# Two transposed probability tiles in one buffer, moved by four transfers, and the first gate weights loaded ahead of the late input rows

## The chip, the cores and the metric

The kernel runs on one core of one Trainium2 chip. The time is that of the device in microseconds (us); the kernel before takes 1884.54 us, the median of three runs (1883.9 to 1887.2). The engines named below are TensorE (PE), which does the matmuls, VectorE (DVE), ScalarE (ACT), GpSimd (POOL) and SyncE (SP), which issues nearly all DMA transfers from one queue, in order.

## The reference

One layer of an encoder is applied to two groups, "prompt" and "sample", of 1024 positions and 1024 channels each, with the same weights. All is in float32.

```
h    = rms_norm(x) * (1 + scale) + shift          # scale, shift, gate from silu(c) @ w_ada
proj = h @ w_in                                   # 1024 x 5376, cut into the parts below
# branch A: 8 query heads, 2 key/value heads, 64 wide; norm and rotation of q, k
oa = softmax(qa @ ka.T / 8) @ va  * silu(za)
# branch B: 4 heads, two 64-wide softmax maps each, 128-wide values
p  = softmax(q0 @ k0.T / 8) - lam * softmax(q1 @ k1.T / 8)
ob = rms_norm(p @ vb) * (1 - lam_init) * silu(zb)
merged = sigmoid(ga) * (oa @ w_proj_a) + sigmoid(gb) * (ob @ w_proj_b)
y = x + gate * (merged @ w_out)
```

## The kernel before, in words

Weights are split into a high part (rounded to the matmul's type, a step of ScalarE, L208) and a remainder (VectorE, L209), and most products are made of several matmuls of such parts. A buffer pool `st` of three tiles receives the weights from memory.

The program takes the prompt group (g = 0) and then the sample group (g = 1). Each has these stages, told with the times of the profiled execution for the prompt group: an opening with the input's norm, keys and values (0 to 130 us; in the sample group the input is normed earlier, behind the end of the prompt group, in `ht_gen`), branch A's attention (131 to 455), branch B's (510 to 808), and the merge with the output projection (about 771 to 972). The sample group's attention stages are at 1054 to 1340 and 1396 to 1714, and its output ends the program. While a stage of attention runs, projections of the next stage and the gate projections (`z_gen`) run beside it: they are matmuls L670 and L881 in the profile, and they fill TensorE while the softmax goes through the other engines. The merge is L1170 and the output L1201.

A **unit** of attention treats two tiles of 128 queries. A unit of branch A has two scores, one tile of probabilities for each of two heads; two units are needed for one mixing (`a_values`, L984). A unit of branch B has four, two maps for each of two query tiles, and is mixed by itself (`b_values`, L1021). For each score (`softmax_unit`) TensorE writes 128 x 1024 scores into one of two banks `s` (L908, L909), VectorE takes the row maximum (L910), ScalarE scales it (L911) and takes the exponential into a tile `p` (L912), which frees the bank. In branch B, VectorE combines the two maps (L952) with a factor `r` (L939, L940). In `flip`, VectorE transposes `p` in blocks of 32 x 32 (L953), and SP then issues four DMA transfers (L958, `q<-p`) that put the four groups of 32 partitions in their places in a tile `q`, from which TensorE takes the transposed probabilities. There are five buffers `p` of 4 KB a partition and two buffers `q` of 8 KB. The pool `p` also serves the opening, the gate loads of the merge (`p<-zd`, L1161), `ht_gen` and a few rows.

What sets the order: `weave` takes steps from several generators by their progress, with numbers from the tables at the top of the file (`ATT_W`, `IN_A`, `Z_A`, `LAST_ATT`, `TAIL` and others), and this gives the program order. A scheduler that simulates the program's timeline then places each instruction on its engine. Some instructions have a priority (`high_priority`, with `QUARTER_P` for instance). On the chip each engine works through its own list in that order.

In the opening, L109 is the line of a helper that keeps instructions in the order in which they are written. The late rows of the input (`load_xT0(1)`) are read there, and the weights of the first gate (`load_w`, into two tiles `u`), behind them.

## Time and profile before

| | us |
|---|---|
| median of three runs | 1884.54 |
| the profiled execution | 1887.84 |
| its span | 1885.6 |
| TensorE busy | 1852.3 (98%) |
| VectorE busy | 1228.1 (65%) |
| ScalarE busy | 843.1 (45%) |

The profiled execution's own time is the span and 2.24 us that lie around it. A view of waits has a row for each pair of waiting line and releaser: total us, times, and the longest. A timeline has start, duration, engine, line, operation, output and inputs, and in brackets the idle time before it with what ended it; `x4` is a run of four instructions that are shown as one. For SP a DMA row is the time of its issue, not of the transfer. In the list of DMA issues the last number is the median us from issue to landing.

### The profile page before, as it was taken

The numbers are of one execution on the slowest core, as the hardware profiler recorded it, in microseconds if no ns is written. First come the engines' busy times: TensorE is split into PE (matmuls) and PEld (weight loads), VectorE is DVE, ScalarE is ACT, GpSimd is POOL, SyncE is SP. The second block draws the span as 40 slices with busy tenths as digits, with TensorE's granted clock in tenths as the row PEclk, the third lists the DMA queues.
The fourth block names the chain that finished last, engine by engine and source line by source line (L and its number), as shares of the span: only waits on it lengthen the run. The fifth ranks groups of instructions, "written<-read, shape, count | busy, mean of one in ns | idle before, by whom it ended". The sixth has DMA issues, their size and how long they took to land.

```text
span 1885.6 us, 32132 instructions
## 1 busy us (share of the span) xinstructions
PE 1852.3 (98%) x11516; PEld 1599.4 (85%) x11516; DVE 1228.1 (65%) x1904; ACT 843.1 (45%) x1801; POOL 364.2 (19%) x692
## 2 busy tenths in 40 slices
PE   9999999999999999999999999999999999999999
PEld 7888888877889998788889888888888989877887
DVE  4756776465478677877464777666547767786731
ACT  3544554443456555524223555444445545552210
POOL 0342200011335152100134210000233513210000
PEclk9999999999999999999999999999999999999999
DMA  9225676676254536887531467776524344579532
GB/s 333 83 72 138 162 201 180 173 215 166 71 134 105 130 91 182 254 286 236 190 122 51 127 180 197 196 181 179 158 78 121 98 107 115 156 230 302 168 106 78
DMA packets 277612, 299.54 MB, mean 159 GB/s; under 512 B 37648, under 2 KB 228304, under 8 KB 277456
## 3 DMA queue, kind: packets, MB, share of 16 engines
q1 hardware_dynamic: 277456, 297.51, 55.6%
q8 instruction: 92, 1.51, 0.3%
q14 instruction: 64, 0.52, 0.1%
HBM read 137.91 MB, written 42.04 MB: 95 GB/s over the span
## 4 chain that ended last, share of the span: by engine, by line
PE 76%; DMA 7%; DVE 7%; SPq 3%; issue 3%; POOL 2%; ACT 2%; DVEq 0%; ACTq 0%; POOLq 0%
PE f L881 21%; PE f L670 18%; PE f L1201 6%; PE a L984 6%; PE f L1170 5%; PE s L908 5%; PE s L909 5%; PE a L1021 4%; PE s L1201 3%; DMA row<-zd 2%; PE s L1170 2%; DVE m L910 2%; SPq L958 1%; SPq L109 1%; DMA st<-in_w_in_dram 1%
## 5 line engine op out<-in xcount | busy, mean ns | idle before, releaser
L881 PE MATMUL f<-u,w 128*128 128x512 f32 x2088 | 524.9, 394 | 0.3 <-DVE u L733 0.3
L670 PE MATMUL f<-w,u 128*128 128x256 f32 x3264 | 448.2, 285 | 0.3 <-ACT ev L863 0.3
L881 PEld LDWEIGHTS f<-u,w 128*128 128x128 f32 x2088 | 382.7, 188 | 76.0 <-PE f L730 0.7
L670 PEld LDWEIGHTS f<-w,u 128*128 128x128 f32 x3264 | 425.2, 191 | 18.4 <-issue 1.4
L910 DVE TENSOR_REDUCE m<-s 128x1 f32<-128x1024 f32 x256 | 309.7, 1218 | 112.6 <-PE s L909 110.6
L953 DVE STREAM_TRANSPOSE p<-p 128x1024 f32<-128x1024 f32 x192 | 238.5, 1242 | 45.8 <-ACT p L912 42.1
L909 PE MATMUL s<-u,sw 128*128 128x512 f32 x512 | 202.9, 398 | 0.0
L209 DVE TENSOR_TENSOR w<-st,w 128x512 fp32r<-128x512 f32 x184 | 123.3, 699 | 82.4 <-ACT w L208 81.8
L208 ACT ACTIVATE w<-st 128x512 fp32r<-128x512 f32 x184 | 107.6, 626 | 133.5 <-DMA st<-in_w_in_dram 60.6
L912 ACT ACTIVATE p<-s,m,rsA 128x1024 f32<-128x1024 f32 x128 | 154.4, 1206 | 5.7 <-DMA q<-p 2.2
L912 ACT ACTIVATE p<-s,m,rsB 128x1024 f32<-128x1024 f32 x128 | 154.4, 1206 | 4.0 <-DMA q<-p 0.5
L695 POOL TENSOR_TENSOR rsB<-ss,nhalf 128x4 f32<-128x4 f32 x64 | 66.4, 1038 | 457.0 <-DVE ss L694 442.7
L1170 PE MATMUL f<-u,w 128*128 128x512 f32 x588 | 142.4, 391 | 0.2 <-DVE u L1181 0.2
L1021 PE MATMUL a<-q,u 128*128 128x256 f32 x512 | 126.1, 388 | 7.5 <-DMA q<-p 4.1
L1170 PEld LDWEIGHTS f<-u,w 128*128 128x128 f32 x588 | 109.9, 188 | 23.6 <-DVE u L1181 0.6
L984 PE MATMUL a<-q,u 128*64 128x128 f32 x2048 | 121.8, 276 | 4.0 <-DMA q<-p 3.9
L984 PEld LDWEIGHTS a<-q,u 128*64 128x64 f32 x2048 | 113.2, 138 | 14.6 <-issue 13.3
L733 DVE TENSOR_TENSOR u<-f,u 64x256 fp32r<-64x256 f32 (+1 forms) x208 | 83.7, 407 | 62.8 <-ACT u L732 57.5
L1021 PEld LDWEIGHTS a<-q,u 128*128 128x128 f32 x512 | 96.6, 194 | 23.0 <-issue 5.3
L1201 PE MATMUL f<-u,w 128*128 128x512 f32 x480 | 111.2, 389 | 0.0
L909 PEld LDWEIGHTS s<-u,sw 128*128 128x128 f32 x512 | 96.6, 189 | 16.2
L908 PE MATMUL s<-u 128*128 128x512 f32 x256 | 107.2, 421 | 2.6 <-ACT p L912 2.5
(208 smaller groups left out, 2152.1 us busy)
## 6 DMA issues: line engine op xcount, KB each, us to landing
q<-p SPq DMA_DIRECT2D x768, 128.0 KB, 2.8
st<-in_w_in_dram SPq DMA_DIRECT2D x128, 256.0 KB, 3.2
zd<-ev SPq DMA_DIRECT2D x96, 256.0 KB, 2.3
sw<-u SPq DMA_DIRECT2D x256, 64.0 KB, 2.1
p<-zd SPq DMA_DIRECT2D x64, 256.0 KB, 5.1
u<-in_w_ada_dram SPq DMA_DIRECT2D x16, 512.0 KB, 8.8
od<-oo SPq DMA_DIRECT2D x64, 128.0 KB, 2.6
st<-in_w_in_dram SPq DMA_DIRECT2D x64, 128.0 KB, 2.9
```

The source lines that it names most:

```text
L209: nc.vector.tensor_tensor(out=wl, in0=st, in1=wh.bitcast(F32), op=ALU.subtract)
L670: nc.tensor.matmul(ps, lt[c][:, sl], w[c][:, wi, :], start=(k == 0), stop=(k == 23))
L881: nc.tensor.matmul(ps, w[c][:, wi, e * P : (e + 1) * P], rt[c], start=(k == 0), stop=(k == 23),)
L908: nc.tensor.matmul(s[:, sl], q, k[:, sl], start=True, stop=False)
L909: nc.tensor.matmul(s[:, sl], sw, k[:, sl], start=False, stop=True)
L910: nc.vector.tensor_reduce(out=m, in_=s, axis=AX.X, op=ALU.max, negate=True)
L912: nc.scalar.activation(pt.rearrange("p (j c a) -> p j c a", j=4, c=8), s.rearrange("p (c a j) -> p j c a", c=8, j=4), AF.Exp, scale=rs, bi ...
L953: nc.vector.transpose(pt, pt)
L984: nc.tensor.matmul(acc[e * 64 : e * 64 + 64, n * P : n * P + P], u["v"](k), blocks[n][:, e, k], start=(k == 0 and n == 1), stop=(k == 7 an ...
L1021: nc.tensor.matmul(acc, u["v"][:, k], pT[:, k], start=(k == 0), stop=(k == 7))
L1170: nc.tensor.matmul(ps, w[:, c, wi, d * P : (d + 1) * P], o[:, oi, :], start=(k == 0), stop=(k == 11))
L1201: nc.tensor.matmul(ps, w[c][:, wi, e * P : (e + 1) * P], m[:, mi, :], start=(k == 0), stop=(k == 23))
```

## The change

There are now two buffers `p` of 8 KB (`p2tile`) and one single buffer `p1` of 4 KB. The two tiles of a unit (in branch B those of the first map, which also receive the combination) share one `p` buffer, laid out as 4 x 2 x 256; the second map of branch B goes into `p1`. The exponential writes with a stride, the transposition reads and writes with one, and `flip` issues nothing for the first tile; after the second, four transfers of 256 KB move both. So there are 384 transfers `q<-p`, not 768, and 863 rows on SP, not 1021. The helpers that used single `p` tiles take halves or quarters of a pair; the gate loads of the merge are issued four at once, one branch's into a `u` tile and the other's into a `p` pair (32 `u<-zd` and 32 `p<-zd` rather than 64 `p<-zd`). In the opening, three loads of the first gate's weights stand ahead of the late rows. The tables have other numbers. The matmuls are the same in number and shape. In the changed file the same places have other line numbers: L908 is L941, L912 is L945, L958 is L994, L984 is L1020, L1021 is L1057, L1170 is L1207, L764 is L797, L868 is L901, L991 is L1027, L208 is L215.

```diff
@@ -41,31 +41,31 @@
 Z_HEAD = (7, 6)
 Z_HEAD_A = (-0.216, -0.32)
 ATT_W = (
-    (0.893, 1.067, 1.068, 1.192, 1.03, 1.769),
-    (1.237, 1.862, 1.041, 1.418, 0.645, 1.256),
+    (0.893, 1.067, 1.068, 1.192, 0.961, 1.769),
+    (1.237, 1.635, 1.041, 1.418, 0.645, 1.256),
 )
 IN_A = (
-    (0.205, -0.07, 0.861, 0.05, 0.25, 0.15),
-    (0.125, -0.05, 0.368, 0.3, -0.03, 0.694),
+    (0.205, -0.07, 1.273, 0.05, 0.25, 0.15),
+    (0.125, -0.05, 0.435, 0.3, -0.03, 0.694),
 )
 Z_A = (
-    (0.2, 0.05, 0.62, -0.05, -0.1, -0.05),
+    (0.153, 0.05, 1.012, -0.05, -0.1, -0.05),
     (-0.215, 0.07, 0.2, 0.16, -0.3, -0.1),
 )
-LAST_ATT = (46, 40)
+LAST_ATT = (48, 40)
 LAST_FILL = (20, 25)
-GATED_A = (0.063, -0.144)
-LATE_A = 1.197
-QUARTER_P = 202
+GATED_A = (0.056, -0.144)
+LATE_A = 1.154
+QUARTER_P = 200
 KV_STEPS = 12
 GATE_AT = 6
 FIRST_ATT = 12
-FIRST_A = 0.26
-TAIL = (3, 3)
-TAIL_A = (0.92, 1.2)
+FIRST_A = 0.349
+TAIL = (1, 4)
+TAIL_A = (0.904, 1.2)
 LAG = 2
-Z_FIRST = (12, 6)
-Z_FIRST_A = (0.017, -0.452)
+Z_FIRST = (14, 4)
+Z_FIRST_A = (-0.106, -0.452)
 CUTS = (3, 6)
@@ -118,7 +118,8 @@
     upool = ent(tc.tile_pool(name="upool", bufs=15))
     wpool = ent(tc.tile_pool(name="wpool", bufs=2))
     spool = ent(tc.tile_pool(name="spool", bufs=3))
-    ppool = ent(tc.tile_pool(name="ppool", bufs=5))
+    ppool = ent(tc.tile_pool(name="ppool", bufs=2))
+    p1pool = ent(tc.tile_pool(name="p1pool", bufs=1))
     qpool = ent(tc.tile_pool(name="qpool", bufs=2))
     tpool = ent(tc.tile_pool(name="tpool", bufs=2))
     mpool = ent(tc.tile_pool(name="mpool", bufs=2))
@@ -162,14 +163,20 @@
         us = [[chunks4(utile()) for _ in range(2)] for _ in range(2)]
         return [[us[s][c // 4][:, c % 4] for c in range(NCH)] + [us[s]] for s in range(2)]
+    def p2tile():
+        return ppool.tile([P, 2048], F32, tag="p", name=nm("p"))
+
     def ptile():
-        return ppool.tile([P, 1024], F32, tag="p", name=nm("p"))
+        return p1pool.tile([P, 1024], F32, tag="p1", name=nm("p1"))
     def pair(dt=F32):
         return qpool.tile([P, 2048], dt, tag="q", name=nm("q"))
     def halves(pt):
         return pt[:, :1024], pt[:, 1024:]
+
+    def fours(pt):
+        return [pt[:, i * 512 : i * 512 + 512] for i in range(4)]
     def halves2(pt):
         return pt[:, :512], pt[:, 512:]
@@ -220,7 +227,7 @@
         w = wpool.tile([P, NCH, 2, 256], F32R, tag="w", name=nm("w"))
         w = [w[:, q * 2 : q * 2 + 2] for q in range(4)]
-        sts = [x.rearrange("p (c n) -> p c n", c=2) for _ in range(2) for x in halves2(ptile())]
+        sts = [x.rearrange("p (c n) -> p c n", c=2) for x in fours(p2tile())]
         def load(q):
             src = mat[q * 256 : (q + 1) * 256, col : col + 256]
@@ -229,6 +236,15 @@
         return ([w[c // 2][:, c % 2] for c in range(NCH)], (w, sts)), load
     def load_w(pieces, room=None):
+
+        return drain_last(load_w_steps(pieces, room))
+
+    def drain_last(steps):
+        for w in steps:
+            pass
+        return w
+
+    def load_w_steps(pieces, room=None):
         if room is None:
             w = wpool.tile([P, NCH, 2, 256], F32R, tag="w", name=nm("w"))
@@ -236,7 +252,9 @@
         else:
             us = [u.rearrange("p (c s n) -> p c s n", c=4, s=2) for u in room]
             w = [u[:, i : i + 2] for u in us for i in (0, 2)]
-        for q in range(4):
+        sts = []
+
+        def load(q):
             st = spool.tile([P, 2, 256], F32, tag="st", name=nm("st"))
             off = 0
             for src in pieces(q):
@@ -244,8 +262,17 @@
                 (dma_next if room else dma)(st[:, :, off : off + n], src.rearrange("(c p) n -> p c n", p=P))
                 off += n
             assert off == 256
-            split_w(w, q, st)
-        return [w[c // 2][:, c % 2] for c in range(NCH)]
+            sts.append(st)
+
+        if room:
+            for q in range(3):
+                load(q)
+            yield
+        for q in range(4):
+            if q == len(sts):
+                load(q)
+            split_w(w, q, sts[q])
+        yield [w[c // 2][:, c % 2] for c in range(NCH)]
     def w_cols(mat, *cols):
         def pieces(q):
@@ -458,6 +485,8 @@
             wts += [load_ada(n) for n in (2 * q, 2 * q + 1)]
             k_load(q)
             q_load(q)
+        z_first = load_w_steps(w_cols(w_in, (z_col(Z_ORDER[0]), 256)), room=(utile(), utile()))
+        next(z_first)
         xT.append(load_xT0(1))
         bank = ps_a.tile([P, 512], F32, tag="a", name=nm("a"))
@@ -501,7 +530,7 @@
                     sums_early(ht, c, 1)
                     if part is not None:
                         ps, part = ada_sum(part), None
-        kva_w.append((load_w(w_cols(w_in, (z_col(Z_ORDER[0]), 256)), room=(utile(), utile())),))
+        kva_w.append((drain_last(z_first),))
         sq = late_squares(xT[1])
         return lambda: inv_rms(sq, pe), lambda rs: start_late(ht, xT[1], rs)
@@ -618,7 +647,9 @@
     def ht_gen(g, ht):
         ss = const.tile([P, NTT], F32, name="ssx")
         for tt in range(NTT):
-            xt = ptile()
+            if tt % 2 == 0:
+                xts = halves(p2tile())
+            xt = xts[tt % 2]
             dma(xt, x_sample[tt * P : (tt + 1) * P])
             nc.scalar.activation(sbank(), xt, AF.Square, accum_out=ss[:, tt : tt + 1])
             if tt % 2:
@@ -637,7 +668,9 @@
         for hf in range(2):
             ht[hf] = new_h()
         for c in range(NCH):
-            xt = ptile()
+            if c % 2 == 0:
+                xts = halves(p2tile())
+            xt = xts[c % 2]
             dma(xt, xT_in[g][c * P : (c + 1) * P])
             for hf in range(2):
                 xh = xt[:, hf * 512 : (hf + 1) * 512]
@@ -679,7 +712,7 @@
     def row_early():
         if not spare:
-            spare.extend(halves2(ptile()))
+            spare.extend(fours(p2tile()))
         return spare.pop(0)
     def rows(ps, nh, rs):
@@ -910,7 +943,7 @@
         nc.vector.tensor_reduce(out=m, in_=s, axis=AX.X, op=ALU.max, negate=True)
         nc.scalar.activation(m, m, AF.Copy, scale=rs)
         nc.scalar.activation(
-            pt.rearrange("p (j c a) -> p j c a", j=4, c=8), s.rearrange("p (c a j) -> p j c a", c=8, j=4),
+            pt.rearrange("p j (c a) -> p j c a", c=8), s.rearrange("p (c a j) -> p j c a", c=8, j=4),
             AF.Exp, scale=rs, bias=m, accum_out=su,
         )
@@ -918,8 +951,11 @@
         if "sw" not in u:
             u["sw"] = swapped(u)
-        pt = ptile()
+        if i == 0:
+            u["p"] = p2tile()
+        both = u["p"].rearrange("p (j t f) -> p t j f", j=4, t=2)
         if "j" in u:
+            pt = both[:, i]
             qt = u["qt"]
             t = qt % 2
             softmax_unit(
@@ -930,6 +966,7 @@
             return i
         t, m = i // 2, i % 2
         qt = u["pr"] * 2 + t
+        pt = ptile().rearrange("p (j f) -> p j f", j=4) if m else both[:, t]
         su = u["su"][:, qt : qt + 1] if m == 0 else tiny.tile([P, 1], F32, tag="su", name=nm("su"))
         softmax_unit(u["q"][m][:, qt * P : (qt + 1) * P], u["rs"](qt, m), u["sw"][:, m, t * P : (t + 1) * P], u["k"][m], pt, su)
         if m == 0:
@@ -951,11 +988,10 @@
             _, p1, f = u[t]
             nc.vector.scalar_tensor_tensor(out=pt, in0=p1, scalar=f, in1=pt, op0=ALU.mult, op1=ALU.add)
         nc.vector.transpose(pt, pt)
-        if t == 0:
+        if t:
             u["pT"] = pair(F32R)
-        dst = u["pT"].bitcast(F32).rearrange("p (i t f) -> p i t f", i=4, t=2)
-        for i in range(4):
-            dma(dst[:, i, t], pt[i * 32 : i * 32 + 32])
+            for i in range(4):
+                dma(u["pT"].bitcast(F32)[:, i * 512 : i * 512 + 512], u["p"][i * 32 : i * 32 + 32])
     def pT_pieces(u):
@@ -1155,13 +1191,14 @@
                 md = st["md"][half, hf]
                 for d in range(4):
                     dt_ = half * 4 + d
+                    if d == 0:
+                        gg = chunks4(p2tile() if br else utile().bitcast(F32))
+                        for a in range(4):
+                            dma(gg[:, a, :], st["gbd" if br else "gad"][(dt_ + a, hf)])
                     if d % 2 == 0:
-                        gg = ptile().rearrange("p (a n) -> p a n", a=2)
-                        for a in range(2):
-                            dma(gg[:, a, :], st["gbd" if br else "gad"][(dt_ + a, hf)])
                         if br:
                             mT[hf].append(utile().rearrange("p (c s n) -> p c s n", c=2, s=2))
-                    g = gg[:, d % 2, :]
+                    g = gg[:, d, :]
                     ps = gbank()
                     k = 0
                     for c in range(4):
```

The order on SP in the opening, before (`u<-in_xT` are the late rows, `st<-in_w_in` the gate weights):

```order
L109 DMA p_191<-in_w_in_dram 128x2x256
L109 DMA p_194<-in_w_in_dram 128x2x256
L109 DMA u_223<-in_xT_prompt_dram 128x2x512 x2
L109 DMA u_224<-in_xT_prompt_dram 128x2x512 x2
L109 DMA st_620<-in_w_in_dram 128x2x256
L109 DMA st_624<-in_w_in_dram 128x2x256
L109 DMA st_628<-in_w_in_dram 128x2x256
L583 DMA tab_653<-in_cosA_dram 128x8x64
L583 DMA tab_655<-in_sinA_dram 128x8x64
L109 DMA st_632<-in_w_in_dram 128x2x256
```

and of the change:

```order
L109 DMA p_193<-in_w_in_dram 128x2x256
L109 DMA p_195<-in_w_in_dram 128x2x256
L109 DMA st_226<-in_w_in_dram 128x2x256
L109 DMA st_228<-in_w_in_dram 128x2x256
L109 DMA st_230<-in_w_in_dram 128x2x256
L109 DMA u_232<-in_xT_prompt_dram 128x2x512 x2
L109 DMA u_233<-in_xT_prompt_dram 128x2x512 x2
L612 DMA tab_654<-in_cosA_dram 128x8x64
L612 DMA tab_656<-in_sinA_dram 128x8x64
L109 DMA st_633<-in_w_in_dram 128x2x256
```

The three weights have moved from behind the rows to ahead of them.

The order on SP in the prompt group's branch A, before, at the moves that are issued from 286.56 us in the trace (`q<-p` with the numbers of the unit's tiles; `od<-oo` stores mixed values, `zd<-ev` a gate):

```order
L958 DMA q_2927<-p_2916 128x1x256
L991 DMA od_131<-oo_2913 128x256
L958 DMA q_2860<-p_2849 128x1x256
L958 DMA q_2927<-p_2916 128x1x256
L958 DMA q_2860<-p_2865 128x1x256
L958 DMA q_2860<-p_2849 128x1x256
L958 DMA q_2927<-p_2916 128x1x256
L958 DMA q_2860<-p_2865 128x1x256
L958 DMA q_2860<-p_2849 128x1x256
L958 DMA q_2927<-p_2937 128x1x256 x3
L958 DMA q_2927<-p_2916 128x1x256
L958 DMA q_2927<-p_2937 128x1x256
```

and of the change, at the same two units:

```order
L901 DMA zd_2966<-ev_2963 128x512
L994 DMA q_2800<-p_2778 128x1x512 x4
L1027 DMA od_134<-oo_2837 128x256
L797 DMA sw_3040<-u_1622 64x256 x2
L797 DMA sw_3040<-u_1623 64x256 x2
L994 DMA q_2866<-p_2840 128x1x512 x4
L901 DMA zd_3082<-ev_3079 128x512
```

Before, the issues of two units (q_2860 and q_2927) are mixed with each other; now the four of each (q_2800 and q_2866) stand together, with other transfers between them.

The order on TensorE in the sample group's branch B, at the second and third scores of its last unit, before (L908 and L909 are scores, L1170 the merge):

```order
L909 MATMUL s_17634<-u_16217,sw_17450 128x512
L908 MATMUL s_17634<-u_16217 128x512
L909 MATMUL s_17634<-u_16217,sw_17450 128x512
L1170 MATMUL f_17612<-u_17338,w_17591 128x512
L908 MATMUL s_17710<-u_16216 128x512
L909 MATMUL s_17710<-u_16216,sw_17450 128x512
L908 MATMUL s_17710<-u_16216 128x512
L909 MATMUL s_17710<-u_16216,sw_17450 128x512
L1170 MATMUL f_17645<-u_17092,w_17591 128x512 x6
```

and of the change (L941 and L942 the scores, L1207 the merge):

```order
L942 MATMUL s_17144<-u_15760,sw_16958 128x512
L941 MATMUL s_17144<-u_15760 128x512
L942 MATMUL s_17144<-u_15760,sw_16958 128x512
L1207 MATMUL f_17122<-u_16850,w_17099 128x512
L1207 MATMUL f_17155<-u_16609,w_17099 128x512 x5
L1079 MATMUL f_17179<-ones_c,at_17136 128x1 x2
L1207 MATMUL f_17155<-u_16609,w_17099 128x512
L1207 MATMUL f_17155<-u_16850,w_17099 128x512 x6
L941 MATMUL s_17211<-u_15759 128x512
L942 MATMUL s_17211<-u_15759,sw_16958 128x512
L941 MATMUL s_17211<-u_15759 128x512
L942 MATMUL s_17211<-u_15759,sw_16958 128x512
```

Between the two scores shown there was one matmul of the merge; there are now thirteen and two small ones.

## The prediction

> **What bounds the kernel now.** I read the page first, then the waits by engine, and last the timeline around the longest waits.
>
> ```profile
> span 1885.6 us, 32132 instructions
> PE 1852.3 (98%) x11516; PEld 1599.4 (85%) x11516; DVE 1228.1 (65%) x1904; ACT 843.1 (45%) x1801; POOL 364.2 (19%) x692
> PE a L1021 <- DMA q<-p: 4.1, 3, 2.7
> PE a L984 <- DMA q<-p: 3.9, 2, 2.3
> PE s L908 <- ACT p L912: 3.8, 4, 1.6
> PE f L730 <- POOL row L719: 2.9, 4, 1.1
> PE a L1021 <- DVE r L939: 2.9, 1, 2.9
> PE f L109 <- ACT row L109: 2.4, 2, 1.7
> ```
>
> TensorE is busy for 98% of the span, so the kernel is bound by its matmuls, and no edit here adds or removes a matmul. What can change is the time in which TensorE stands still, and its clock. The rows of the second group give total us, number of times and the longest. The largest are waits for the moves of the probabilities (q<-p, 4.1 and 3.9, and the 2.9 put down to r, at 1701.81, where the move is as late), for exponentials that free a score bank (3.8), and for the table rows of the opening. All the idle gaps that I counted on TensorE come to about 29 us. The second loss is the clock, in a view by windows whose columns are the window, its length, busy us and instructions of five engines, then the granted clock, the DMA share and GB/s:
>
> ```profile
> 50.75:54.16 3.41, 3.41 (x10) 2.65 (x9) 3.17 (x7) 3.41 (x7) 0.00 (x0) 0.50 0.48 139
> 122.43:125.84 3.41, 3.41 (x17) 3.31 (x16) 1.69 (x5) 1.44 (x4) 0.00 (x0) 0.50 0.61 109
> 299.93:303.34 3.41, 3.36 (x32) 3.39 (x34) 0.42 (x1) 0.00 (x0) 0.00 (x0) 0.50 0.68 190
> 303.34:306.75 3.41, 3.41 (x42) 3.01 (x40) 0.92 (x2) 0.94 (x2) 0.00 (x0) 1.00 0.79 237
> 781.21:784.62 3.41, 3.41 (x9) 2.69 (x10) 2.93 (x4) 2.11 (x4) 0.34 (x1) 0.50 0.88 279
> 1702.80:1706.21 3.41, 3.41 (x10) 2.70 (x9) 1.93 (x3) 0.82 (x3) 0.00 (x0) 0.50 0.97 350
> ```
>
> Behind the waits near 48, 120, 300, 781 and 1702 the clock is 0.50 for 3.41 us; the row from 303.34 shows 1.00 right after. Such a stretch costs half its length, 1.7 us. So a wait of 1.7 to 2.9 us costs 3.4 to 4.6 us when it draws a slow stretch. The stretch at 122.43 I leave as it is. All losses together are 29 + 5 × 1.7 = 37.5 us: the most that any reordering can win.
>
> [...]
>
> **The change part by part.** First the **moves**. One transposed tile went out in four issues; now two tiles share a buffer and go out in four issues of twice the bytes, once the second is transposed.
>
> ```profile
> L958 SPq DMA_DIRECT2D q<-p x768: 542/602/1864, 135.3 to 1721.7; - x192
> L953 DVE STREAM_TRANSPOSE p<-p x192: 1217/1245/1248, 134.0 to 1716.1; 128x1024 f32<-128x1024 f32 x192
> L912 ACT ACTIVATE p<-s,m,rsA x128: 1186/1207/1212, 131.5 to 1338.7; 128x1024 f32<-128x1024 f32 x128
> q<-p SPq DMA_DIRECT2D x768, 128.0 KB, 2.8
> zd<-ev SPq DMA_DIRECT2D x96, 256.0 KB, 2.3
> st<-in_w_in_dram SPq DMA_DIRECT2D x128, 256.0 KB, 3.2
> p<-zd SPq DMA_DIRECT2D x64, 256.0 KB, 5.1
> ```
>
> 384 issues fewer at 0.602 us free SP's in-order queue of 231 us. That queue isn't on the path except where several moves stand back to back. A 256 KB move isn't in this trace; its landing lies between 2.3 and 5.1 us by the other 256 KB transfers, and I take 3.2, the weights' value, since it also spreads over the DMA engines as 2.8 us for 128 KB does. First issue to last landing is then 3 × 0.6 + 3.2 = 5.0, and with 0.5 for the queue 5.5 us. The transposition (1.245) and the exponential (1.207) have new strides, the same element counts; I add nothing, and bound it by 0.1 us each, which DVE at 65% and ACT at 45% hide.
>
> ```profile
> 286.56 2.58 SPq L958 DMA_DIRECT2D q<-p  x4
> 289.06 1.25 DVE L953 STREAM_TRANSPOSE p<-p 128x1024 f32<-128x1024 f32 x1 [0.69 <-ACT p L912]
> 289.24 1.21 ACT L912 ACTIVATE p<-s,m,rsA 128x1024 f32<-128x1024 f32 x1
> 289.83 7.68 SPq L958 DMA_DIRECT2D q<-p  x12
> 295.99 1.21 ACT L912 ACTIVATE p<-s,m,rsA 128x1024 f32<-128x1024 f32 x1 [1.77 <-DMA q<-p]
> 299.98 1.42 PE L984 MATMUL a<-q,u 128*64 128x128 f32 x10 [2.35 <-DMA q<-p]
> ```
>
> In the **first branch A** sixteen issues of two units stand here in one row, mixed, from 286.56 to 297.5. The mixing matmul at 299.98 waits 2.35 us for the last but few of them. Afterwards the first unit's four can go from 286.56, and the second's from 290.4, when its last transposition (289.06 + 1.25) is done; they land by 290.4 + 5.5 = 295.9, ahead of 297.6 (299.98 - 2.35), when TensorE arrives. That removes 2.35 and its slow stretch, 1.7. The other wait of this kind (3.9 - 2.35 = 1.55, near 420) goes for the same reason, but by the same sum with no room to spare, so I count 1.3. Together **-5.3**; bounds -5.6 (both, in full) and 0 (both remain).
>
> In **branch B** the first tile no longer goes out while the second is computed. The last landing comes later: four issues of 256 KB after the second transposition, 0.4 us by landing (3.2 against 2.8), up to 2.3 (5.1 against 2.8).
>
> ```profile
> 774.64 1.24 DVE L953 STREAM_TRANSPOSE p<-p 128x1024 f32<-128x1024 f32 x1
> 775.90 2.54 SPq L958 DMA_DIRECT2D q<-p  x4
> 781.12 1.11 PE L1021 MATMUL a<-q,u 128*128 128x256 f32 x2 [2.65 <-DMA q<-p]
> 615.39 2.54 SPq L958 DMA_DIRECT2D q<-p  x4
> 621.60 0.59 PE L1021 MATMUL a<-q,u 128*128 128x256 f32 x2
> ```
>
> At 781.12 and the three other places of the first group that wait on q<-p or beside it (four in all) I take 0.5 each, **+2.0**. Places with room lose room: at 621.60 the second tile's issues start 6.2 us ahead, of which 4.8 are used. There the order of the changed kernel also leaves less between the unit's last score and its mixing: 16 wide and 56 narrow matmuls (16 × 0.227 + 56 × 0.12 = 10.4 us at the pitch of the trace) in place of 44 and 32 (13.8). The second unit of that stage goes from 65 and 21 (17.3) to 54 and 8 (13.2). Taken whole, these two places would wait 2 to 3 us each with 1.7 for the clock, 8.5 together; if the exponentials move up with them, nothing. I take **+2.7**, nearer to nothing, since the planner that places them puts the scores and moves of that unit elsewhere too.
>
> ```profile
> 1688.65 0.69 DVE L1133 TENSOR_TENSOR row<-row,row 128x512 f32<-128x512 f32 x1 [3.31 <-DMA row<-zd]
> 1692.19 0.50 PE L908 MATMUL s<-u 128*128 128x512 f32 x1 [1.63 <-ACT p L912]
> 1694.50 0.50 PE L908 MATMUL s<-u 128*128 128x512 f32 x1 [0.88 <-ACT p L912]
> ```
>
> In the **last branch B** the scores wait for exponentials, because VectorE, in order, stood 3.31 us for a gate row that SP had issued among moves; the row maximum was queued behind it. Afterwards the second and third score there are thirteen matmuls of 0.23 us apart rather than one, and half as many issues stand before the rows. Of the 3.8 us of this kind I count half, **-1.9** (bounds 0 and -3.8 with one clock stretch).
>
> The **buffers** add a wait: an exponential of unit n+2 now writes into the buffer of unit n, and must wait until all four moves of n have landed, where five single tiles rotated before. The row at 295.99 (1.77 us) shows such a wait already. At 289.24 an exponential ran while the moves two units back started at 286.56; with the pair it could start only at 286.56 + 5.5 = 292.1, 2.8 us later. Behind it in ACT's queue stand the gate and evacuation work, and behind these TensorE's banks. Two score banks take about 2 us of this. Over the stages the margin of unit n+2 against the landing of n lies between -5 and +6 us; with landings 2 us earlier it is around nought. I count **+1.5** for the few places beyond cover (4 of 63 for the single buffer of the second map, by 0.8 to 1.4).
>
> [...]
>
> The **opening**. The weights of the first gate are loaded ahead of the late input rows.
>
> ```profile
> 34.39 3.24 SPq L109 DMA_DIRECT2D u<-in_xT_prompt_dram  x4
> 37.99 2.60 SPq L109 DMA_DIRECT2D st<-in_w_in_dram  x3
> 47.16 0.63 ACT L208 ACTIVATE u<-st 128x512 fp32r<-128x512 f32 x1 [6.86 <-DMA st<-in_w_in_dram]
> 48.33 1.05 PE L109 MATMUL f<-two,row 128*128 128x2 f32 x8 [1.73 <-ACT row L109]
> 52.38 2.18 ACT L109 ACTIVATE q<-u 128x512 f32<-128x512 f32 x4
> ```
>
> ScalarE stood 6.86 us for a weight, and behind it stood the row on which TensorE waited 1.73. The weights were issued 3.6 us after the rows and landed at 47.16; issued first, they land 4 to 5.5 us earlier, and ScalarE is free in time. The rows land some 1.5 us later, near 48.4, and are first read at 52.38, so that side is covered by 4 us. **-3.4** (1.73 and the clock, 1.7); bounds -3.4 and, if the cover went, +1. The gate loads of the merge, four at a time, hide behind matmuls as before. The remaining small waits, some 10 us in dozens of places, fall or move with a lighter queue; I take **-1.6**, bounds -5 and +5.
>
> **Sum**: -3.4 - 5.3 + 2.0 + 2.7 - 1.9 + 1.5 - 1.6 = **-6.0 us**. The profiled execution took 1887.84 us (the span and 2.2 around it), 3.3 above the median of the runs, 1884.54. I carry the difference over to the median: about **1878.5 us**, by itself 1871 to 1885.
>
> **The rivals.**
>
> *All the moves get out in time.* Also the waits at 781, 823, 1681 and 1702 go (4.1 + 2.9), with two clock stretches (3.4), and B's landings cost nothing: -6.0 - 2.0 - 2.7 - 4 = -15, **1869 us**. For it: the order was laid out anew and every q<-p wait is of 0.7 to 2.9 us. Against: in B the trace has the second tile's moves on the path, and these become larger.
>
> *The waits only move.* TensorE's 29 us of gaps lie in dozens of places, and a reordering of all of them gives each a new draw; savings in the opening and A are paid back in B (leads whole, 8.5 instead of 2.7): about **1884 us**. For it: of 1885.6 us no one wait is more than 0.16%.
>
> *The pair buffers hold ScalarE.* In the two A stages, 62 units, the exponential waits for the landing two units back. In the trace it starts up to 5 us ahead of that landing at about half of them. If the scores can't be held by two banks for more than 2 us, half of the units (31) wait 0.5 us or more each, 16 us, or 10 if few draw the slow clock, against -6.0 - 1.5 saved: -7.5 + 16 = +8, **1893 us**. It decides from the point where the exponentials wait more than 2 us longer than before at most units. For it: 289.24. Against: the moves land earlier by as much, and many of the tiles wait for their q buffer long after they are transposed.
>
> *The moves don't gain.* If a 256 KB move lands like the gate loads (5.1), the four issues take 6.9 us to the last landing, little less than the eight; then A keeps 0.8 of 5.3, and B's four places cost 2.3 each, not 0.5: -6.0 + 4.5 + 7.2 = +5.7, **1890 us**. It is the value of one kind of row in three.
>
> **How the numbers follow.** My sum 0.38; all moves in time 0.20; waits only move 0.22; pair buffers 0.15; no gain 0.05. What a measurement tells from no change is about 0.2%, 3.8 us: faster is below 1880.8, slower above 1888.3. Of my sum (1871 to 1885) three quarters are faster, 0.28, with 0.10 the same; the first rival gives 0.20, the second 0.06 faster, 0.13 the same and 0.03 slower; the third 0.02 the same and 0.13 slower; of the last 0.02 is the same and 0.03 slower. Faster 0.54, same 0.27, slower 0.19. The range, 1865 to 1891, takes in the first rival with some of its own spread and reaches to the third.
>
> **What would show it.** Right, if in the profile after: no clock of 0.50 near 51 and 300; no ScalarE wait of 6.86 us near 47; no wait on q<-p at the mixing of branch A; about 384 moves whose landing is near 3.2 us; waits of a few us in B near 560 and 620. Wrong, if ScalarE's p tiles show waits on q<-p beyond the 5.7 us that they have now with TensorE waiting for s behind them, if the landing is above 4 us, or if the matmuls' own busy time changes by more than the clock explains.

## The result: 6.4% slower, and the profile after

The changed kernel takes 2005.12 us (median of five runs, 2001.68 to 2008.12), the kernel before 1884.54 beside it. The ratio is 1.0639, with a 95% interval of 1.0623 to 1.0655. Forecast were 1878.5 us and a range of 1865 to 1891.

The page of the changed kernel (span, engines, the chain of work, three groups of instructions with busy us, mean ns and the idle time ahead of them, and two rows of the DMA issues):

```profile
span 1999.6 us, 31348 instructions
PE 1882.7 (94%) x11516; PEld 1618.7 (81%) x11516; DVE 1229.3 (61%) x1904; ACT 841.2 (42%) x1801; POOL 368.2 (18%) x692
PE 57%; DMA 17%; SPq 11%; DVE 7%; issue 4%; ACT 3%; POOL 2%; DVEq 0%; ACTq 0%; POOLq 0%
L1020 PE MATMUL a<-q,u 128*64 128x128 f32 x2048 | 135.0, 295 | 54.8 <-DMA q<-p 53.0
L945 ACT ACTIVATE p<-s,m,rsA 128x1024 f32<-128x1024 f32 x128 | 154.2, 1205 | 69.8 <-DMA q<-p 54.7
L1057 PE MATMUL a<-q,u 128*128 128x256 f32 x512 | 132.9, 404 | 31.0 <-DMA q<-p 30.5
q<-p SPq DMA_DIRECT2D x384, 256.0 KB, 4.8
zd<-ev SPq DMA_DIRECT2D x96, 256.0 KB, 3.2
```

Its view of waits for TensorE (total us, times, longest):

```profile
PE a L1020 <- DMA q<-p: 53.0, 26, 4.2
PE a L1057 <- DMA q<-p: 30.5, 16, 3.9
PE s L941 <- ACT p L945: 6.8, 7, 3.0
```

and one row of the same view for SP, at the issues of the moves:

```profile
SPq L994 <- DMA q<-p: 40.7, 19, 3.3
```

The span is 114 us longer. TensorE's idle time went from 29 to 112 us (the gaps of its matmuls, summed), and 83.5 of it are two rows: there are 42 waits of mixings for the moved probabilities, where there were five. TensorE's busy time grew by 30.4 us with the same matmuls: the clock is granted at 0.50 in sixteen stretches of 3.4 or 6.8 us, 71.7 us in all, rather than in five of 17.1 us in all. Half of that difference is 27 of the 30 us. 83 and 30 are the whole loss. ScalarE's exponentials also wait for q<-p, 54.7 us against 2.2, and SP itself stands behind moves that have not landed. The exponential and the transposition with their new strides take 1205 and 1242 ns, as before (1206 and 1242).

One mixing in each branch shows how it comes about; these are rows of the changed kernel's timeline, SP's rows being issues:

```profile
1207.19 3.38 SPq L797 DMA_DIRECT2D sw<-u  x4
1208.03 1.25 DVE L990 STREAM_TRANSPOSE p<-p 128x1024 f32<-128x1024 f32 x1 [0.56 <-ACT p L945]
1210.67 4.22 SPq L994 DMA_DIRECT2D q<-p  x4
1219.66 3.71 PE L1020 MATMUL a<-q,u 128*64 128x128 f32 x64 [1.99 <-DMA q<-p]
...
807.50 1.24 DVE L990 STREAM_TRANSPOSE p<-p 128x1024 f32<-128x1024 f32 x1
808.77 4.45 SPq L994 DMA_DIRECT2D q<-p  x4
817.47 5.88 PE L1057 MATMUL a<-q,u 128*128 128x256 f32 x13 [3.74 <-DMA q<-p]
```

The four moves stand on SP within 0.1 us of the transposition in branch B and 1.4 after it in this unit of branch A. Then 8.7 to 9.0 us pass until TensorE can go on. The forecast had 5.5. In the windows of that wait (length, five engines, clock, DMA share, GB/s), and of the slow stretch behind it:

```profile
808.77:817.33 8.56, 4.95 (x22) 3.75 (x20) 7.07 (x11) 3.81 (x8) 2.20 (x3) 0.95 0.85 226
816.44:823.27 6.83, 5.80 (x14) 4.67 (x15) 4.22 (x6) 3.33 (x7) 0.00 (x0) 0.50 0.83 265
```

the DMA engines are busy for 85% of the time and move 226 GB/s; in the kernel before, the window from 781.21 us has 279 GB/s at 88%. Busy engines at a lower rate suggest that the moves themselves are slow, and not only late in the queue. That is the question for the experiments.

### The profile page after: what moved, and what is told of

It is laid out like the page before. It is cut to its first block, busy times and chain, and to the rows that moved or that the text cites. A ratio compares the mean times of both kernels' runs of the same rounds, so it can differ in the third digit from the quotient of the medians.

```text
span 1999.6 us, 31348 instructions
## 1 busy us (share of the span) xinstructions
PE 1882.7 (94%) x11516; PEld 1618.7 (81%) x11516; DVE 1229.3 (61%) x1904; ACT 841.2 (42%) x1801; POOL 368.2 (18%) x692
## 4 chain that ended last, share of the span: by engine, by line
PE 57%; DMA 17%; SPq 11%; DVE 7%; issue 4%; ACT 3%; POOL 2%; DVEq 0%; ACTq 0%; POOLq 0%
PE f L703 13%; PE f L914 11%; DMA q<-p 11%; PE a L1020 6%; SPq L994 6%; PE f L1238 5%; PE f L1207 5%; PE a L1057 4%; PE s L1238 3%; PE s L941 3%; PE s L942 3%; DVE m L943 3%; SPq L797 2%; DMA st<-in_w_in_dram 2%; PE s L1207 2%
## 5 line engine op out<-in xcount | busy, mean ns | idle before, releaser
L914 PE MATMUL f<-u,w 128*128 128x512 f32 x2088 | 533.0, 396 | 5.2 <-DVE u L766 3.0
L990 DVE STREAM_TRANSPOSE p<-p 128x1024 f32<-128x1024 f32 x192 | 238.3, 1242 | 113.4 <-ACT p L945 96.0
L942 PE MATMUL s<-u,sw 128*128 128x512 f32 x512 | 202.3, 399 | 0.0
L1020 PE MATMUL a<-q,u 128*64 128x128 f32 x2048 | 135.0, 295 | 54.8 <-DMA q<-p 53.0
L945 ACT ACTIVATE p<-s,m,rsA 128x1024 f32<-128x1024 f32 x128 | 154.2, 1205 | 69.8 <-DMA q<-p 54.7
L215 ACT ACTIVATE w<-st 128x512 fp32r<-128x512 f32 x184 | 106.6, 625 | 179.1 <-DMA st<-in_w_in_dram 89.5
L1020 PEld LDWEIGHTS a<-q,u 128*64 128x64 f32 x2048 | 126.9, 150 | 65.9 <-issue 52.4
L1057 PE MATMUL a<-q,u 128*128 128x256 f32 x512 | 132.9, 404 | 31.0 <-DMA q<-p 30.5
L945 ACT ACTIVATE p<-s,m,rsB 128x1024 f32<-128x1024 f32 x128 | 154.3, 1205 | 4.1 <-DVE p L989 0.6
L1207 PE MATMUL f<-u,w 128*128 128x512 f32 x588 | 143.2, 392 | 1.3 <-DVE u L1179 0.6
L1057 PEld LDWEIGHTS a<-q,u 128*128 128x128 f32 x512 | 100.7, 203 | 52.3 <-issue 36.6
L1207 PEld LDWEIGHTS f<-u,w 128*128 128x128 f32 x588 | 109.5, 188 | 25.6 <-DVE ssB L1081 1.2
L941 PE MATMUL s<-u 128*128 128x512 f32 x256 | 108.3, 427 | 4.8 <-ACT p L945 4.7
L942 PEld LDWEIGHTS s<-u,sw 128*128 128x128 f32 x512 | 97.3, 190 | 17.3 <-issue 0.6
L1238 PE MATMUL f<-u,w 128*128 128x512 f32 x480 | 111.2, 389 | 0.0
```

Of the source, the lines that this page charges most:

```text
L914: nc.tensor.matmul(ps, w[c][:, wi, e * P : (e + 1) * P], rt[c], start=(k == 0), stop=(k == 23),)
L941: nc.tensor.matmul(s[:, sl], q, k[:, sl], start=True, stop=False)
L942: nc.tensor.matmul(s[:, sl], sw, k[:, sl], start=False, stop=True)
L945: nc.scalar.activation(pt.rearrange("p j (c a) -> p j c a", c=8), s.rearrange("p (c a j) -> p j c a", c=8, j=4), AF.Exp, scale=rs, bias=m, ...
L990: nc.vector.transpose(pt, pt)
L1020: nc.tensor.matmul(acc[e * 64 : e * 64 + 64, n * P : n * P + P], u["v"](k), blocks[n][:, e, k], start=(k == 0 and n == 1), stop=(k == 7 an ...
```

## The experiments

The table holds all kernels; "landing" is the page's median for one q<-p, "unit" the median from a unit's first issue to its last landing, "A" and "B" the median from the end of a unit's second transposition to that landing in each branch (from the transposition's end and those landings that the trace tells, 209 of 384 in the changed kernel), and "waits" the two rows of TensorE on q<-p together. Where a unit has eight moves, the first four start ahead of its second transposition, so that "unit" is longer than the moves themselves; e13 alone holds all eight back. The kernels e1 to e7, e9 to e11, e13 and e14 were each run once, e8, e12, e15 and e16 seven, eleven, four and four times.

| kernel | us | landing | unit | A | B | waits |
|---|---|---|---|---|---|---|
| before | 1884.5 | 2.8 | 8.8 | 7.8 | 4.9 | 8.0 |
| changed | 2005.1 | 4.8 | 8.1 | 10.6 | 7.9 | 83.5 |
| e1 eight early | 1909.4 | 2.8 | | 8.3 | 4.8 | 4.9 |
| e2 eight late | 1907.6 | 2.8 | | 7.5 | 5.1 | 6.9 |
| e3 straight | 1876.5 | 2.5 | 4.5 | 6.3 | 4.5 | 3.7 |
| e4 singles late | 1884.4 | 2.8 | | 9.4 | 5.0 | 6.2 |
| e5 old tables | 2000.4 | 4.8 | | | | 70.9 |
| e6 three pairs | 2015.8 | 4.8 | 8.1 | 9.7 | 8.1 | 84.8 |
| e7 two queues | 2004.5 | 6.1 | | | | 63.9 |
| e8 opening only | 1893.2 | 2.8 | | | | 3.3 |
| e9 spread source | 1877.7 | 2.5 | 4.6 | 6.4 | 4.6 | 3.3 |
| e10 order 0213 | 1969.9 | 4.8 | 7.6 | 9.7 | 7.6 | 61.9 |
| e11 two queues 0213 | 1971.3 | 6.0 | | | | 55.9 |
| e12 before 0213 | 1883.5 | 2.8 | | | | 6.1 |
| e13 eight held back | 1926.0 | 2.8 | 7.6 | 13.5 | 7.5 | 5.4 |
| e14 spread in a half | 1970.1 | 4.4 | 7.3 | 9.7 | 7.0 | 63.3 |
| e15 pairs only | 1903.9 | 2.8 | | 7.2 | 4.9 | 4.3 |
| e16 tables only | 1911.0 | 2.8 | | 8.1 | 5.1 | 6.4 |

### Burst, buffers, or the shape of a transfer: e1 to e4

e1 is the changed kernel with

```diff
-        if t:
+        if t == 0:
             u["pT"] = pair(F32R)
-            for i in range(4):
-                dma(u["pT"].bitcast(F32)[:, i * 512 : i * 512 + 512], u["p"][i * 32 : i * 32 + 32])
+        dst = u["pT"].bitcast(F32).rearrange("p (i t f) -> p i t f", i=4, t=2)
+        for i in range(4):
+            dma(dst[:, i, t], pt[i * 32 : i * 32 + 32])
```

> The changed kernel (pair buffers, new tables, new opening) with eight transfers of 128 KB again, each tile's four issued right after its own transposition. Theory 1, the burst: 1 MB that starts only after the second transposition takes 7.7 us to its last landing where the second tile's 0.5 MB took 4.9 before; then the mixings' waits on q<-p (83 us in the changed kernel) fall under 25 us and the time is 1885 to 1915 us. Theory 2, the pair buffers: an exponential still waits for both tiles' landing two units back, so ScalarE's idle time on q<-p at the p tiles (55 us) stays above 30 us and the time is 1930 to 1985 us. Theory 3, the order by the new tables: unchanged, 1985 us or more.

It took 1909.4 us, and the kernel before 1885.8 beside it. 96 of the 120 us are back, and the waits at the mixings are gone (4.9). ScalarE's waits on q<-p, though, are still 31.1 us, as its page shows:

```profile
L945 ACT ACTIVATE p<-s,m,rsA 128x1024 f32<-128x1024 f32 x128 | 154.3, 1206 | 52.7 <-DMA q<-p 31.1
```

The pair buffers do hold it, and TensorE hardly feels it. So theory 2 is out as the cause of the large loss.

e2 issues the same eight transfers in the branch for the second tile:

```diff
-            for i in range(4):
-                dma(u["pT"].bitcast(F32)[:, i * 512 : i * 512 + 512], u["p"][i * 32 : i * 32 + 32])
+            dst = u["pT"].bitcast(F32).rearrange("p (i t f) -> p i t f", i=4, t=2)
+            src = u["p"].rearrange("p (j t f) -> p t j f", j=4, t=2)
+            for tt in range(2):
+                for i in range(4):
+                    dma(dst[:, i, tt], src[i * 32 : i * 32 + 32, tt])
```

> The changed kernel with eight transfers of 128 KB, all issued after the second transposition: as late as the pair's four, in smaller pieces. Theory 1, as lateness and bytes: first issue to last landing stays at 7 to 8 us (8 x 0.6 issue and 2.8), and the time is 1985 to 2015 us. If it is the size of a transfer that is bad (256 KB from 32 partitions lands in 4.8 us against 2.8), the time falls to 1930 to 1960 us. Theories 2 and 3: 1985 to 2015 us too.

1907.62 us, below every case that was written down. But the run did not test what it was meant to: in the trace half of each unit's transfers in branch B start ahead of the second transposition (median 7.9 us ahead of its end), since the scheduler puts each tile's transfers where that tile is ready. The same holds for e4, the kernel before with

```diff
-        if t == 0:
+        if t:
             u["pT"] = pair(F32R)
-        dst = u["pT"].bitcast(F32).rearrange("p (i t f) -> p i t f", i=4, t=2)
-        for i in range(4):
-            dma(dst[:, i, t], pt[i * 32 : i * 32 + 32])
+            dst = u["pT"].bitcast(F32).rearrange("p (i t f) -> p i t f", i=4, t=2)
+            for tt in range(2):
+                for i in range(4):
+                    dma(dst[:, i, tt], u[tt][0][i * 32 : i * 32 + 32])
```

> The kernel before (five single buffers, old tables, old opening) with the one edit that the first tile's four transfers of 128 KB wait for the second tile's transposition, so that eight are issued together. Theory 1 (lateness): waits on q<-p of 40 us or more at the mixings, time 1940 to 2000 us. Theory 2 (an exponential waits for a pair to land) and theory 3 (the new tables): little, 1880 to 1910 us.

1884.43 us, no change from 1885.8; lateness stayed untested until e13.

e3 keeps every instruction of the changed kernel in its place and alters what a transfer reads:

```diff
-                dma(u["pT"].bitcast(F32)[:, i * 512 : i * 512 + 512], u["p"][i * 32 : i * 32 + 32])
+                dma(u["pT"].bitcast(F32)[:, i * 512 : i * 512 + 512], u["p"][:, i * 512 : i * 512 + 512])
```

> The changed kernel in the same order of instructions, but each of the four 256 KB transfers copies a block of 512 columns of all 128 partitions straight to the same place, rather than 2048 columns of 32 partitions: the same bytes and the same 2 KB pieces, read from four times as many partitions. The rearrangement of the probabilities is left out by this, so the outputs are others. If the 32 source partitions limit the rate, the landing falls from 4.8 to 3.3 us or less, the last of four to 5.5 us after the first issue, and the time to 1900 to 1940 us. If the DMA engines limit it whatever the partitions, the landing stays above 4.3 us and the time above 1980 us. Theory 2 (the buffers) gives less than half of the loss back in either case: above 1945 us.

1876.46 us, 9 below the kernel before and 129 below the changed one. The moves in its page:

```profile
q<-p SPq DMA_DIRECT2D x384, 256.0 KB, 2.5
```

Same order on each engine, same buffers, same bytes, same 2 KB pieces: one transfer lands in 2.5 us, not 4.8, four in 4.5, not 8.1. The whole loss, and more, hangs on where a transfer reads: from 32 partitions, or from all 128.

### What of the change does not matter to it: e5, e6

e5 is the changed kernel with the old numbers in all tables:

```diff
-    (0.893, 1.067, 1.068, 1.192, 0.961, 1.769),
+    (0.893, 1.067, 1.068, 1.192, 1.03, 1.769),
...
-Z_FIRST = (14, 4)
+Z_FIRST = (12, 6)
```

> The changed kernel with the table numbers of the kernel before. Theory R, the rate (a move of 256 KB from 32 partitions runs at some 220 GB/s, so that the four of a pair land 7.7 us after the first issue, and the same order with quick moves took 1876 us): the tables hardly matter, 1980 to 2025 us. Theory T, that the new numbers suit only quick moves: 1900 to 1950 us.

2000.4 us: the tables are not it. e6 has a third pair buffer, and one tile u less to make room:

```diff
-    upool = ent(tc.tile_pool(name="upool", bufs=15))
+    upool = ent(tc.tile_pool(name="upool", bufs=14))
-    ppool = ent(tc.tile_pool(name="ppool", bufs=2))
+    ppool = ent(tc.tile_pool(name="ppool", bufs=3))
```

> The changed kernel with three pair buffers rather than two (and 14 tiles u rather than 15, to make room). Theory R in its plain form, that a mixing simply stands behind the landing of its own pair: ScalarE's idle time on q<-p at the p tiles (55 us) falls under 15 us, but the mixings' waits (83 us) stay above 60 us and the time at 1975 to 2005 us. Theory L, that the loop through the buffers (landing, exponential two units on, its transposition, its landing) makes the loss: the waits at the mixings fall under 35 us and the time to 1895 to 1935 us.

2015.84 us, 11 above the changed kernel and above the 1975 to 2005 that theory R had; the tile u that is missing may cost these. Branch A's exponentials now wait 0.2 us on q<-p (54.7 before the third buffer), and the mixings wait 84.8 us, as they did with two:

```profile
L945 ACT ACTIVATE p<-s,m,rsA 128x1024 f32<-128x1024 f32 x128 | 154.1, 1204 | 3.7 <-DMA q<-p 0.2
```

The loop through the buffers that I had put up as theory L, because the first exponential of a unit starts in the trace right as the moves two units back land, is not what costs: each mixing stands behind the landing of its own pair.

### Which partitions, and whether others can be read beside them: e7, e9, e10, e11, e14

e9 reads 32 partitions that stand four apart, 8 KB from each as in the changed kernel:

```diff
-                dma(u["pT"].bitcast(F32)[:, i * 512 : i * 512 + 512], u["p"][i * 32 : i * 32 + 32])
+                dma(u["pT"].bitcast(F32)[:, i * 512 : i * 512 + 512], u["p"][i::4])
```

> The changed kernel in the same order, but each of the four transfers reads 32 partitions that stand four apart (0, 4, 8, ... and so on) instead of 32 neighbours: as many partitions, bytes and 2 KB pieces, 8 KB from each partition. The rearrangement is thereby another, and so are the outputs. Theory P: 32 neighbouring partitions are reached through half of the paths only, so that the rate is halved; then the landing falls to 2.8 us or less and the time to 1870 to 1895 us, as with the straight copy. Theory Q: a partition gives its bytes at a limited rate, and 32 of them are too few wherever they lie; then the landing stays above 4.3 us and the time above 1975 us.

1877.71 us, landing 2.5: as quick as the straight copy. So 32 partitions are not too few; it matters which they are. e14 takes them two apart within one half of the 128:

```diff
             for i in range(4):
-                dma(u["pT"].bitcast(F32)[:, i * 512 : i * 512 + 512], u["p"][i * 32 : i * 32 + 32])
+                lo = i // 2 * 64 + i % 2
+                dma(u["pT"].bitcast(F32)[:, i * 512 : i * 512 + 512], u["p"][lo : lo + 63 : 2])
```

> As with the sources four partitions apart (same order, another rearrangement, other outputs), but each transfer reads 32 partitions two apart within one half: 0, 2, ... 62, then 1, 3, ... 63, then the same in the upper half. If each half of the partitions has its own paths, a transfer still sees half of them: landing 4.5 us or more, 1960 us or more. If each group of 32 has its own, it sees two groups: landing 2.5 to 3.2 us and 1875 to 1905 us.

1970.05 us and a landing of 4.4: of the 2.3 us that e9 takes off a landing, spreading within one half brings 0.4, and in time 35 of the 127 us. Most of the gain needs both halves; why even this much comes within one is open. The page of e9, engines and moves:

```profile
PE 1847.6 (99%) x11516; PEld 1596.1 (85%) x11516; DVE 1229.1 (66%) x1904; ACT 841.9 (45%) x1801; POOL 371.0 (20%) x692
q<-p SPq DMA_DIRECT2D x384, 256.0 KB, 2.5
```

its window from one unit's first issue on, in branch B near the place shown above:

```profile
767.25:771.80 4.55, 3.83 (x17) 2.52 (x15) 4.55 (x7) 3.43 (x7) 0.00 (x0) 1.00 0.89 327
```

and the moves in the page of e14:

```profile
q<-p SPq DMA_DIRECT2D x384, 256.0 KB, 4.4
```

In e9 the DMA engines move 327 GB/s at a share of 0.89, against 226 at 0.85 in the changed kernel. A transfer that reads from both halves of the 128 partitions landed in 2.5 us (e3, e9), one that stays in one half in 4.4 (e14) or 4.8 (the changed kernel). The paths by which theory P accounts for this are my guess; no run shows a path by itself.

Can two halves be read at once? e10 issues the groups of the changed kernel in another order:

```diff
-            for i in range(4):
+            for i in (0, 2, 1, 3):
```

e7 has GpSimd issue groups 1 and 3, and e11, in the order of e10, groups 2 and 3 (`i > 1` for `i % 2`):

```diff
-                dma(u["pT"].bitcast(F32)[:, i * 512 : i * 512 + 512], u["p"][i * 32 : i * 32 + 32])
+                (nc.gpsimd.dma_start if i % 2 else dma)(u["pT"].bitcast(F32)[:, i * 512 : i * 512 + 512], u["p"][i * 32 : i * 32 + 32])
```

> The changed kernel with the four transfers issued in the order of groups 0, 2, 1, 3; the instructions stand where they stood and outputs are right. Theory P with the upper and lower 64 partitions on different paths: neighbours in the queue then use different paths and overlap, the last landing comes under 6.5 us after the first issue (7.7 before) and the time falls to 1900 to 1960 us. If each DMA engine takes one transfer after the other without overlap, or by theory Q, nothing changes: above 1985 us.

> The changed kernel with the second and fourth transfer of each pair issued by GpSimd, the first and third by SP, so that two queues feed the DMA engines and two groups of 32 partitions are read at once. If the rate is limited by the group of 32 partitions that all engines read from at one time, the last landing comes 5.5 us or less after the first issue and the time falls to 1895 to 1940 us. If the DMA engines are limited for this kind of move whatever is read beside, the landing stays above 7 us and the time above 1975 us. If GpSimd's issues are slow (over 1.5 us each), it is slower than 2005 us.

> As with two queues before (groups 1 and 3 on GpSimd), but now GpSimd issues groups 2 and 3 and SP groups 0 and 1, so that what is read at the same time lies in different halves of the partitions. Theory P with halves on different paths: the last landing comes at 5.5 us or less after the first issue (8.5 with the other pairing) and the time is 1890 to 1940 us. Otherwise as the other pairing: 1990 to 2015 us.

e10: 1969.9 us, a unit's moves in 7.6 us rather than 8.1. That is a sixth of what e9 gains there (0.57 of 3.55), in time 35 of 120 us, below what I expected of overlap. e7: 2004.47 us, each transfer slower (6.1) and a unit's moves in 8.6 us. e11: 1971.31, as e10 with one queue. A second queue gained nothing here (2004.47 us against 2005.12, and 1971.31 against 1969.9). The 0.5 us that a unit's moves gain in e10 could be a little overlap of neighbours in the queue that read from different halves; no run shows such an overlap by itself, and e14 gained as much without that order. A rearrangement that is right and reads from both halves in one transfer wasn't tried: its pattern would have to step over partitions in a second dimension.

e12 makes the exchange of e10, and nothing else, in the kernel before.

> The kernel before with the four transfers of each tile issued in the order of groups 0, 2, 1, 3 and nothing else. [...] Without overlap of halves: ratio 0.999 to 1.001.

1883.48 us, ratio 0.9993 (0.9983 to 1.0003), the landing 2.8 as before: no change that can be told. That there was little to gain is my estimate from two figures of this case: an issue of 128 KB takes SP 0.602 us (the median of 768), which is 218 GB/s, near the 226 of the window above.

### Late, or late without being planned for: e13

e13 keeps eight transfers of 128 KB in program order on SP, the second tile's first, so that none can start ahead of the second transposition:

```diff
-            for i in range(4):
-                dma(u["pT"].bitcast(F32)[:, i * 512 : i * 512 + 512], u["p"][i * 32 : i * 32 + 32])
+            dst = u["pT"].bitcast(F32).rearrange("p (i t f) -> p i t f", i=4, t=2)
+            src = u["p"].rearrange("p (j t f) -> p t j f", j=4, t=2)
+            for tt in (1, 0):
+                for i in range(4):
+                    dma_next(dst[:, i, tt], src[i * 32 : i * 32 + 32, tt])
```

> The changed kernel with eight transfers of 128 KB per pair that are kept in program order on SP, the second tile's four first, so that none starts before the second transposition. If lateness is the loss in branch B (landing 7.9 us after the second transposition in the changed kernel, 4.9 in the kernel before), it stays near 7.7 here (8 x 0.6 + 2.9), the waits of B stay above 20 us and the time is above 1945 us. If the size of a transfer from 32 partitions is the loss, B's waits fall under 12 us and the time is 1895 to 1930 us.

1925.97 us. The landings are nearly as late as in the changed kernel in B (7.5 us after the transposition) and later in A (13.5), and ScalarE waits as long for them (54.9 us), and still the mixings wait only 5.4 us; in its view of waits the larger row is now that of the score banks:

```profile
PE s L941 <- ACT p L945: 11.5, 9, 2.9
PE a L1023 <- DMA q<-p: 3.9, 3, 2.3
```

So a late burst that the order allows for costs 17 us over e1, not 96; my reading that B's waits must stay fell. The difference stands in the order: between a unit's last score and the first matmul of its mixing the changed kernel has, as the median, matmuls for 12.5 and 13.1 us in branch A of the two groups and 16.1 and 15.1 in branch B (their count by the pitch of the trace, 0.227 us for 512 columns, 0.12 for 256 and 0.06 for 128). The kernel before has 12.7, 13.5, 15.9 and 15.0. e13 has 17.2, 17.6, 18.4 and 17.2, which is 2 to 5 us more. So the changed kernel has the room of the kernel before, and its moves take 3 us more. Why e13 got more room is not shown by itself: the scheduler saw eight issues there rather than four, but it also had them as `dma_next`, which ties them to other transfers in program order (in branch A the first of a unit's moves is issued 5.8 us after the second transposition, the median). With the room of the changed kernel and quick moves (e3, e9) the mixings wait 3.7 and 3.3 us in all.

### What the other parts cost: e8, e15, e16

e8 is the kernel before with the new opening alone, the edits of `load_w` and of `start` as the change has them, of which this is a part:

```diff
...
+        z_first = load_w_steps(w_cols(w_in, (z_col(Z_ORDER[0]), 256)), room=(utile(), utile()))
+        next(z_first)
         xT.append(load_xT0(1))
...
```

> The kernel before with the new opening alone: three loads of the first gate's weights ahead of the late rows, tables and buffers as before. By the prediction's term the wait of 1.73 us at the opening and its slow stretch go, -3.4 us: ratio 0.9975 to 0.999. If the rest of the order moves with it, anything within 0.3% of the kernel before; a ratio above 1.003 would say that the opening costs time.

1893.24 us, ratio 1.0041 (1.0030 to 1.0053): 0.4% slower. At the opening itself the 1.73 us became 1.62 at 43.98, on VectorE, and the slow stretch at 50.75 is gone. The order behind it is another throughout, and so are its waits: in its profiled execution, whose span is 9.7 us longer, TensorE's gaps are 3.2 us more, and five stretches at half clock make 30.7 us rather than 17.1; half of that difference, 6.8 us, is lost.

e15 has the buffers of the change alone, with eight transfers as in e1, the old tables and the old opening; e16 the new tables alone in the kernel before. Against the kernel before, e15 and then e16:

```diff
-    ppool = ent(tc.tile_pool(name="ppool", bufs=5))
+    ppool = ent(tc.tile_pool(name="ppool", bufs=2))
+    p1pool = ent(tc.tile_pool(name="p1pool", bufs=1))
...
```
```diff
-    (0.893, 1.067, 1.068, 1.192, 1.03, 1.769),
+    (0.893, 1.067, 1.068, 1.192, 0.961, 1.769),
...
-Z_FIRST = (12, 6)
+Z_FIRST = (14, 4)
```

> The kernel before with the buffers of the change (two pairs and one single, gate loads four at once) but its own tables and opening, and eight transfers, each tile's after its transposition. If the buffers make the rest: ScalarE's p tiles wait 50 us or more on q<-p (62 with new tables, 5.7 before) and the ratio is 1.008 to 1.016. If the tables make it: ratio within 0.3% of one.

> The kernel before with the table numbers of the change and nothing else. If the tables make the rest: ratio 1.008 to 1.016. If the buffers make it: within 0.4% of one, either side, since all waits are drawn anew.

e15: 1903.85 us, ratio 1.0093 (1.0078 to 1.0108), with 80.6 us of waits of the p tiles on q<-p, counted as the 62 of the expectation over all engines; ScalarE's own are 41.9 (31.1 in e1), and the rest is VectorE behind it. e16: 1910.99, ratio 1.0132 (1.0115 to 1.0149). Both were to be apart, one near nothing; each costs some 1% alone, e1 with all three 24 us, and with quick moves all three together gain 7 to 9 (e3 and e9 against the kernel before beside them). They do not add. I take it that the numbers of the tables belong to the buffers and the moves that they were found with; no run shows more than the sums.

## Why the prediction was wrong

**The bound** (TensorE, only its idle time and its clock can change) held: 83 us of idle time and 30 of clock are the difference. That slow stretches come with waits held too, and cost more than counted: there are sixteen, and each begins in a wait of TensorE or up to 1.2 us behind one. The stretch of 6.83 us at half rate above stands at a wait of 3.74 us, and five of 3.41 us in this trace stand at single waits of 2.0 to 2.7 us.

**The step that failed** is "its landing lies between 2.3 and 5.1 us by the other 256 KB transfers, and I take 3.2, the weights' value, since it also spreads over the DMA engines", with "3 × 0.6 + 3.2 = 5.0, and with 0.5 for the queue 5.5 us" for a unit. Measured: 4.8 and 8.1. The last of the four lands 5.5 us after its issue, and it is issued 2.5 us behind the first, not 1.8 (medians); in branch A the first stands another 2.1 us behind the transposition, where e3 has 0.1. The weights' transfer (3.2 us) writes all 128 partitions; this one (4.8 us) reads 32 neighbours. A shape was matched by its bytes and not by its partitions. The row at hand held a warning: 128 KB at 0.602 us for an issue is 218 GB/s, and it could not be excluded that this pace was also the pace of the moves themselves. Halving the issues then asks for twice that.

**-5.3 in branch A** became 53 us of waits. Its arithmetic was right apart from the landing: with quick moves (e9) 0.6 us of wait is left of 3.9, the slow stretch near 300 is gone, and the landing after the transposition is 6.4 us where the sum had 5.5. **+2.0 and +2.7 in branch B** became 30.5; with quick moves 2.7 of waits are left there, so these terms were too dark.

**The opening, -3.4:** ScalarE's 6.86 us went, as worked out (0.45 now, at 41.30), and the slow stretch with it. The wait did not vanish; 0.89 us remain at 44.08, on VectorE's part of the same weights' work, which now stands ahead. -0.84 - 1.7 = -2.5.

In the changed kernel's timeline, and in the window that had the slow stretch:

```profile
41.30 2.13 ACT L215 ACTIVATE u<-st 128x512 fp32r<-128x512 f32 x3 [0.45 <-DMA st<-in_w_in_dram]
44.08 0.74 PE L109 MATMUL s<-w,u 128*128 128x256 f32 x4 [0.89 <-DVE u L109]
```
```profile
50.75:54.16 3.41, 3.41 (x17) 2.80 (x16) 2.70 (x7) 3.32 (x7) 0.00 (x0) 1.00 0.50 162
```

**The tails, -1.9:** not borne out. The changed kernel still waits 2.95 us for a score bank near 1810, and e9 3.5 near 1691.

**The buffers, +1.5:** the wait was real (54.7 us of ScalarE's time, 41.9 in e15), and the rival that priced it at 16 us is near what e15 costs (17 us), though e6 shows that it was not the cause of this loss. With quick moves it is not there: ScalarE waits 2.3 us on q<-p in e9 and 2.7 in the kernel before. The 5.7 us that the prediction gave as ScalarE's are those of all engines at the p tiles.

**The sum** of -6.0 is close to what the same order does with quick moves: 1876.5 and 1877.7 us. So the prediction was that of a kernel with quick moves, which land in 2.5 us in e3 and e9. That the total comes out so close is luck in part: B's terms were too dark, and those of the tails too bright.

**The rival "the moves don't gain"** had nearly the right landing, 5.1, though 6.9 us for a unit rather than 8.1, and 1890 us. Its price was wrong: it charged the four mixings that waited already. The margins between the last landing and the mixing were 0.1 to 3.0 us at 38 of the 45 mixings for which the trace of before tells the landing, and 3 us more at each unit eats most of them: 42 waits of 2 us on average, and the clock. (In the rival "all the moves get out in time" the -4 doesn't follow from its parts, 4.1 + 2.9 + 3.4; with these it would have been 1863 us.)

What would have shown it was named: a landing above 4 us, and ScalarE's waits on q<-p. Both came, but TensorE's waits for a score bank behind ScalarE's grew only from 3.8 to 6.8 us, so the second was not where the time went.

## What to carry to other kernels

Before transfers are made larger, divide their bytes by the time of an issue, and compare the result with a rate that the trace shows for such transfers. Here 128 KB at 0.602 us is 218 GB/s, the window with the larger moves has 226, and with twice the bytes for an issue the landing went from 2.8 to 4.8 us. Look at which partitions a transfer reads, not only at how many: 256 KB from 32 neighbours landed in 4.8 us here, and in 2.5 from 128, or from 32 that are spread over both halves. And where a planner sets the order, a transfer that takes longer than the planner thinks costs its lateness at each place that has no room for it; about the same lateness with more room in the order cost a third of it here (e13 +39 us, the change +120).

## What I had not expected of the hardware

A transfer of 256 KB from 32 neighbouring partitions lands in 4.8 us, the same from 32 partitions four apart in 2.5, and from 32 two apart in one half in 4.4. The order of the four groups in one queue was worth 35 us (e10); a second queue brought nothing (e7, 2004.5 us against 2005.1), and the landing only took longer with it (6.1 us against 4.8). If the moves of the kernel before had little room above SP's own pace, 218 GB/s, none of its waits showed it. What 32 neighbours give at most was measured by no run; the nearest figure is the 226 GB/s of the window, with other traffic in it.
